# Row sums of a 16384 x 1024 array: the last two rows in shared column pieces, one row for each engine, and ScalarE as the engine that stores

## Chip, core and metric

One core of one Trainium2 chip. The metric is device time in microseconds (us), best read as the median of several executions. "Faster" or "slower" would need 2%, that is 3.3 us. In the tables, times inside one execution count from the start of its span, at the first load's issue. The batches of runs were on different chips, by the record, so a time is compared within its batch; the traces are one execution of each kernel.

## The reference

```python
x = np.random.randn(32, 512, 1024).astype(np.float32)
def reference(x):
    return np.sum(x, axis=-1).astype(np.float32)
```

67.1 MB are read, 64 KB are written, and there is one addition for each number read.

## The kernel before

Each of the 128 partitions owns 128 rows, in 8 groups of 16. Groups 0 to 6 are one load each (16 rows of 4 KB, 64 KB for each partition). VectorE (DVE) sums them with one reduce; in group 6 ScalarE (ACT) takes half, with a Copy activation for each row whose accumulator output is the sum and whose elementwise output nobody reads. Group 7 is the tail. It comes in loads of 8, 4, 2, 1 rows and a last row in three column pieces, so that little is left to do when the last byte has landed.

```python
    nbig = J // BIG - 1                       # 7; BIG = 16
    tail = [(8, 4), (4, 2), (2, 1)]           # (rows, rows for ScalarE)
    ...
        def act(dst, src, n):
            nc.scalar.activation(out=scratch[:, :n], in_=src, func=Copy, accum_out=dst)
    ...
        for i in range(nbig):
            t = inpool.tile([P, BIG * dim + 2], fp32)
            rows_of(t, 0, BIG, i * BIG, BIG // 2 if i == nbig - 1 else 0)
            if i % 3 == 2:
                store(nc.gpsimd, i - 2, i + 1)
        store(nc.gpsimd, nbig - 1, nbig)
        ...                                   # loads and sums of 8, 4, 2 rows
        rows_of(t, a, 1, nbig * BIG + a, 1)   # row 14: ScalarE alone
        a += 1
        j = nbig * BIG + a                    # row 15: DVE alone, three pieces
        last = t[:, a * dim :]
        cuts = [0, 384, 768, dim]
        for c0, c1 in zip(cuts, cuts[1:]):
            nc.sync.dma_start(out=last[:, c0:c1], in_=rows_from(j, 1)[:, 0, c0:c1])
        for i, (c0, c1) in enumerate(zip(cuts, cuts[1:])):
            if c1 < dim:                      # partial sum goes right behind the row
                vec(last[:, dim + i : dim + i + 1], last[:, c0:c1])
            else:                             # last piece and both partial sums at once
                vec(sums[:, j : j + 1], last[:, c0 : dim + i])
        store(nc.sync, nbig, nbig + 1)
```

`scratch` is a single tile in SBUF (SBUF and PSUM are two memories on the chip, from which the tile pools take their buffers). The stores of groups 0 to 6 are issued by GpSimd (POOL), the last one by the sync engine (SP).

Of the kernel before, what the change touches and what calls it, by code (L numbers as in the profile page):

```python
# [1 line left out]

# [4 lines left out]


def issue_first_load_at_entry(nc):

    main, *rest = nc.main_func.blocks
    SP = mybir.EngineType.SP
    for block in rest:
        insts = list(block.instructions)
        at = next(
            (k for k, i in enumerate(insts) if isinstance(i, mybir.InstDMACopy) and i.engine == SP),
            None,
        )
        if at is None:
            continue  # L20
        load = insts.pop(at)
        assert not load.sync_info.on_wait
        block.instructions = insts
        entry = list(main.instructions)
        k = next(k for k, i in enumerate(entry) if isinstance(i, mybir.InstDrain) and i.engine == SP)
        main.instructions = entry[:k] + [load] + entry[k:]
        return


@with_exitstack  # L30
def kernel(
    ctx: ExitStack,
    tc: tile.TileContext,
    x: bass.AP,
    out: bass.AP,
):
    nc = tc.nc
    nc.at_finalize(issue_first_load_at_entry)
    fp32 = mybir.dt.float32
    P = 128  # L40
    batch, seq, dim = x.shape
    rows = batch * seq
    J = rows // P
    BIG = 16


    x_g = x.flatten_outer_dims().rearrange("(g p j) d -> g p j d", p=P, j=BIG)
    out_v = out.rearrange("b s -> (b s)").rearrange("(g p j) -> p g j", p=P, j=BIG)

    def rows_from(j, n):  # L50
        return x_g[j // BIG, :, j % BIG : j % BIG + n, :]


    nbig = J // BIG - 1
    tail = [(8, 4), (4, 2), (2, 1)]

    with (
        tc.tile_pool(name="in", bufs=3) as inpool,
        tc.tile_pool(name="scratch", bufs=1) as spool,
        tc.tile_pool(name="stage", bufs=1) as stpool,  # L60
    ):
        sums = stpool.tile([P, J], fp32)
        scratch = spool.tile([P, dim], fp32)

        def vec(dst, src):
            nc.vector.tensor_reduce(  # L66
                out=dst, in_=src, axis=mybir.AxisListType.X, op=mybir.AluOpType.add
            )

        def act(dst, src, n):  # L70
            nc.scalar.activation(  # L71
                out=scratch[:, :n],
                in_=src,
                func=mybir.ActivationFunctionType.Copy,
                accum_out=dst,
            )

        def rows_of(t, a, n, j, n_act):
            nv = n - n_act
            block = t[:, a * dim : (a + n) * dim].rearrange("p (n d) -> p n d", d=dim)  # L80
            nc.sync.dma_start(out=block, in_=rows_from(j, n))  # L81
            if nv:
                vec(sums[:, j : j + nv], block[:, :nv, :])
            for q in range(nv, n):
                act(sums[:, j + q : j + q + 1], block[:, q, :], dim)

        def store(eng, g0, g1):
            eng.dma_start(  # L88
                out=out_v[:, g0:g1],
                in_=sums[:, g0 * BIG : g1 * BIG].rearrange("p (g j) -> p g j", j=BIG),  # L90
            )

        for i in range(nbig):
            t = inpool.tile([P, BIG * dim + 2], fp32)
            rows_of(t, 0, BIG, i * BIG, BIG // 2 if i == nbig - 1 else 0)

            if i % 3 == 2:
                store(nc.gpsimd, i - 2, i + 1)
        store(nc.gpsimd, nbig - 1, nbig)

        t = inpool.tile([P, BIG * dim + 2], fp32)
        a = 0
        for n, n_act in tail:
            rows_of(t, a, n, nbig * BIG + a, n_act)
            a += n


        rows_of(t, a, 1, nbig * BIG + a, 1)
        a += 1
        j = nbig * BIG + a  # L110
        last = t[:, a * dim :]
        cuts = [0, 384, 768, dim]
        for c0, c1 in zip(cuts, cuts[1:]):
            nc.sync.dma_start(out=last[:, c0:c1], in_=rows_from(j, 1)[:, 0, c0:c1])
        for i, (c0, c1) in enumerate(zip(cuts, cuts[1:])):
            if c1 < dim:
                vec(last[:, dim + i : dim + i + 1], last[:, c0:c1])
            else:
                vec(sums[:, j : j + 1], last[:, c0 : dim + i])
        store(nc.sync, nbig, nbig + 1)  # L120


# [1 line left out]
_INS = ['x']  # L124
_OUTS = [((32, 512), 'float32')]


# [23 lines left out]
```

## Time and profile before

Median 162.79 us of 3 runs at first. The profiled execution has a span of 161.5 us.

First the page of the profile: the slice rows (busy share in tenths, 40 equal slices of the span) and the DMA queues (packets, MB, share of 16 engines' span).

```profile
DVE  0000049998699968999499994999949997697883
DMA  8997998997997997996996996996997996999990
q1 hardware_dynamic: 2160, 67.12, 97.1%
q0 software_dynamic: 96, 0.06, 0.1%
```

The load queue (q1) is busy for 97.1% of the span on all sixteen engines. The packet records say the same: the median load packet of 65,536 B takes 2.418 us, which is about 434 GB/s for sixteen engines; the first 16 packets take longer, 3.57 us in the mean. DVE is idle for the first five slices, until the first 16 rows have landed, and waits for loads again later.

Next, the end of the timeline (start us, duration us, engine, line, operation, output<-input, count, and in brackets the idle time before it and what ended it).

```profile
157.09 1.06 ACT L71 ACTIVATE scratch<-t 128x1024 f32<-128x1024 f32 x1
157.64 1.01 DVE L66 TENSOR_REDUCE t<-t 128x1 f32<-128x384 f32 x2 [0.68 <-DMA t<-in_x_dram]
158.06 0.19 ACT L71 ACTIVATION_READ_ACCUMULATOR scratch<-t 128x1 f32 x1
158.68 0.42 DVE L66 TENSOR_REDUCE sums<-t 128x1 f32<-128x258 f32 x1
159.17 0.35 SPq L88 DMA_DIRECT2D out_dram<-sums  x1
```

The second line is two merged reduces, one for each of the first two pieces. Beside it stand the landings by the semaphore records of the same trace (a semaphore is a counter that a transfer or an instruction raises when it is done, and that others wait for): the pieces landed at 157.54, 158.05 and 158.37 us. So the final reduce began 0.31 us after the last landing: DVE was still at the second piece. The final store was issued at 159.17 and landed at 160.59; 0.95 us later the span ends.

The last pieces of the chain of waits (start us, duration us, what) tell the same story from the back: one DMA stretch of 38.6 us, then two partial reduces, then the final one.

```profile
118.95 38.59 DMA t<-in_x_dram
...
157.64 1.02 DVE t L66 x2
158.66 0.02 issue
158.68 0.42 DVE sums L66
```

### The profile page before, as it was taken

How to read it: one execution, taken by the hardware profiler on the slowest of the kernel's cores; microseconds unless marked ns; L12 is line 12 of the kernel's file. 1: busy time of each engine (PE TensorE's matmuls, PEld its weight loads, DVE VectorE, ACT ScalarE, POOL GpSimd, SP SyncE). 2: the span in 40 equal slices, each digit the busy share in tenths (PEclk: the TensorE clock that was granted, in tenths of full speed). 3: DMA queues.
4: the chain of work that ended last, by engine and by line, in shares of the span. 5: the costliest groups of instructions: out<-in, count | busy, mean ns of one | idle time of the engine just before them, and what ended most of it. 6: DMA issues, size and time to landing. Idle time of an engine off the chain costs nothing.

```text
span 161.5 us, 124 instructions
## 1 busy us (share of the span) xinstructions
DVE 121.4 (75%) x13; ACT 19.7 (12%) x33; POOL 2.4 (1%) x7
## 2 busy tenths in 40 slices
DVE  0000049998699968999499994999949997697883
ACT  3000000000000000000000000000000000698891
POOL 0000000000000000000200000000000001001000
DMA  8997998997997997996996996996997996999990
GB/s 260 519 438 341 519 406 373 519 438 341 519 454 325 519 471 308 519 487 292 519 493 293 519 487 292 519 487 292 519 454 325 519 487 292 391 491 389 410 392 14
DMA packets 2256, 67.18 MB, mean 416 GB/s; under 512 B 416, under 2 KB 848, under 8 KB 976
## 3 DMA queue, kind: packets, MB, share of 16 engines
q1 hardware_dynamic: 2160, 67.12, 97.1%
q0 software_dynamic: 96, 0.06, 0.1%
HBM read 67.11 MB, written 0.07 MB: 416 GB/s over the span
## 4 chain that ended last, share of the span: by engine, by line
DMA 74%; DVE 22%; SPq 1%; issue 0%; DVEq 0%
DMA t<-in_x_dram 74%; DVE sums L66 22%; SPq L81 1%; DVE t L66 1%; DVEq L66 0%
## 5 line engine op out<-in xcount | busy, mean ns | idle before, releaser
L66 DVE TENSOR_REDUCE sums<-t 128x16 f32<-128x16384 f32 (+5 forms) x11 | 120.4, 10941 | 37.1 <-DMA t<-in_x_dram 37.0
L71 ACT ACTIVATE scratch<-t 128x1024 f32<-128x1024 f32 x16 | 16.9, 1057 | 137.8 <-DMA t<-in_x_dram 137.3
L88 POOL DMA_DIRECT2D out_dram<-sums x3 | 2.2, 732 | 146.2 <-DVE sums L66 135.4
L71 ACT ACTIVATION_READ_ACCUMULATOR scratch<-t 128x1 f32 x16 | 3.0, 186 | 0.0
L66 DVE TENSOR_REDUCE t<-t 128x1 f32<-128x384 f32 x2 | 1.0, 549 | 0.7 <-DMA t<-in_x_dram 0.7
L71 ACT ACT_TABLE_LOAD x1 | 1.3, 1283 | 0.8 <-PEq L135 0.8
L135 POOL MEMSET const-float32-0.0<- 128x1 f32 x1 | 0.1, 98 | 0.2 <-issue 0.2
L135 POOL MEMSET const-bfloat16-1.0<- 128x1 bf16 x1 | 0.1, 101 | 0.0
L135 POOL MEMSET const-uint8-127<- 128x1 uint8 x1 | 0.1, 99 | 0.0
L135 POOL MEMSET const-float32-1.0<- 128x1 f32 x1 | 0.1, 98 | 0.0
## 6 DMA issues: line engine op xcount, KB each, us to landing
t<-in_x_dram SPq DMA_DIRECT2D x1, 4096.0 KB, 31.2
t<-in_x_dram SPq DMA_DIRECT2D x1, 2048.0 KB, 35.9
t<-in_x_dram SPq DMA_DIRECT2D x1, 1024.0 KB, 37.8
t<-in_x_dram SPq DMA_DIRECT2D x1, 512.0 KB, 38.6
t<-in_x_dram SPq DMA_DIRECT2D x2, 192.0 KB, 38.6
t<-in_x_dram SPq DMA_DIRECT2D x1, 128.0 KB, 38.4
t<-in_x_dram SPq DMA_DIRECT2D x7, 40.8
out_dram<-sums POOLq DMA_DIRECT2D x2, 24.0 KB, 7.9
```

Source lines behind the costliest of these rows:

```text
L66: nc.vector.tensor_reduce(out=dst, in_=src, axis=mybir.AxisListType.X, op=mybir.AluOpType.add)
L71: nc.scalar.activation(out=scratch[:, :n], in_=src, func=mybir.ActivationFunctionType.Copy, accum_out=dst,)
L81: nc.sync.dma_start(out=block, in_=rows_from(j, n))
L88: eng.dma_start(out=out_v[:, g0:g1], in_=sums[:, g0 * BIG : g1 * BIG].rearrange("p (g j) -> p g j", j=BIG),)
L135: nc = _bacc.Bacc("TRN2", target_bir_lowering=False, num_devices=1)
```

## The change

The intent: share the last two rows between the engines, so that both work on the end of the stream at once; take POOL out of the kernel; put the store of groups 1 to 6 where it hides under the end of the tail; and issue a first, early store from ScalarE. The diff, cut to its core:

```diff
-    tail = [(8, 4), (4, 2), (2, 1)]
+    pieces = (640, 256, 128)
-        tc.tile_pool(name="scratch", bufs=1) as spool,
+        tc.tile_pool(name="unread", bufs=4, space=bass.MemoryType.PSUM) as upool,
+        tc.manual_schedule(),
         def act(dst, src, n):
+            unread = upool.tile([P, dim], fp32)
             nc.scalar.activation(
-                out=scratch[:, :n],
+                out=unread[:, :n],
@@ groups 0 to 6
-            if i % 3 == 2:
-                store(nc.gpsimd, i - 2, i + 1)
-        store(nc.gpsimd, nbig - 1, nbig)
+            if g == 1:
+                store(nc.scalar, 0, 1)       # ScalarE's first instruction
@@ tail: 8, 4, 2 rows as before; then, in place of row 14 and row 15
+        for width in pieces:                 # each piece: both rows
+            if len(parts) == k:              # k = 2; room before the last piece
+                at += k
+            part = t[:, at : at + 2 * width].rearrange("p (n d) -> p n d", n=2)
+            nc.sync.dma_start(out=part, in_=rows_from(j, 2)[:, :, c : c + width])
+            ...
+        w = t[:, at - 2 * width - k : at + k]
+        for i, part in enumerate(parts[:k]): # row 14: DVE, row 15: ScalarE
+            vec(w[:, i : i + 1], part[:, 0, :])
+            act(w[:, k + 2 * width + i : k + 2 * width + i + 1], part[:, 1, :], pieces[i])
+        store(nc.scalar, 1, last)
+        vec(sums[:, j : j + 2], w.rearrange("p (n d) -> p n d", n=2))
         store(nc.sync, last, last + 1)
```

In the buffer, DVE's partial sums stand before the last piece of row 14 and ScalarE's behind the last piece of row 15. One reduce of 2 x 130 columns therefore finishes both rows; it has to wait for ScalarE. The change also brings `tc.manual_schedule()`, program order.

More of the change, by code (lines that the diff above doesn't have):

```diff
@@ L51, in rows_from @@
         return x_g[j // BIG, :, j % BIG : j % BIG + n, :]
-    nbig = J // BIG - 1
-    tail = [(8, 4), (4, 2), (2, 1)]
+    last = J // BIG - 1
+    pieces = (640, 256, 128)
     with (
         tc.tile_pool(name="in", bufs=3) as inpool,
-        tc.tile_pool(name="scratch", bufs=1) as spool,
+        tc.tile_pool(name="unread", bufs=4, space=bass.MemoryType.PSUM) as upool,
         tc.tile_pool(name="stage", bufs=1) as stpool,
+        tc.manual_schedule(),
     ):
         sums = stpool.tile([P, J], fp32)
-        scratch = spool.tile([P, dim], fp32)
         def vec(dst, src):
@@ L76, in act, with rows @@
             )
-        def rows_of(t, a, n, j, n_act):
+        def rows(t, a, n, j, n_act):
             nv = n - n_act
@@ L81, in rows_of @@
             nc.sync.dma_start(out=block, in_=rows_from(j, n))
-            if nv:
-                vec(sums[:, j : j + nv], block[:, :nv, :])
+            vec(sums[:, j : j + nv], block[:, :nv, :])
             for q in range(nv, n):
@@ L91, in store @@
             )
-        for i in range(nbig):
-            t = inpool.tile([P, BIG * dim + 2], fp32)
-            rows_of(t, 0, BIG, i * BIG, BIG // 2 if i == nbig - 1 else 0)
-            if i % 3 == 2:
-                store(nc.gpsimd, i - 2, i + 1)
-        store(nc.gpsimd, nbig - 1, nbig)
-        t = inpool.tile([P, BIG * dim + 2], fp32)
+        for g in range(last):
+            t = inpool.tile([P, BIG * dim + 4], fp32)
+            rows(t, 0, BIG, g * BIG, BIG // 2 if g == last - 1 else 0)
+            if g == 1:
+                store(nc.scalar, 0, 1)
+        t = inpool.tile([P, BIG * dim + 4], fp32)
         a = 0
-        for n, n_act in tail:
-            rows_of(t, a, n, nbig * BIG + a, n_act)
+        j = last * BIG
+        for n in (8, 4, 2):
+            rows(t, a, n, j + a, n // 2)
             a += n
-        rows_of(t, a, 1, nbig * BIG + a, 1)
-        a += 1
-        j = nbig * BIG + a
-        last = t[:, a * dim :]
-        cuts = [0, 384, 768, dim]
-        for c0, c1 in zip(cuts, cuts[1:]):
-            nc.sync.dma_start(out=last[:, c0:c1], in_=rows_from(j, 1)[:, 0, c0:c1])
-        for i, (c0, c1) in enumerate(zip(cuts, cuts[1:])):
-            if c1 < dim:
-                vec(last[:, dim + i : dim + i + 1], last[:, c0:c1])
-            else:
-                vec(sums[:, j : j + 1], last[:, c0 : dim + i])
-        store(nc.sync, nbig, nbig + 1)
+        j += a
+        at = a * dim
+        k = len(pieces) - 1
+        parts = []
+        c = 0
+        for width in pieces:
[3 more added lines that the diff above has]
+            nc.sync.dma_start(out=part, in_=rows_from(j, 2)[:, :, c : c + width])
+            parts.append(part)
+            at += 2 * width
+            c += width
+        w = t[:, at - 2 * width - k : at + k]
[4 more added lines that the diff above has]
+        vec(sums[:, j : j + 2], w.rearrange("p (n d) -> p n d", n=2))
+        store(nc.sync, last, last + 1)
 _INS = ['x']
```

## The prediction

> **What bounds it.** The load stream. The slice table has DMA at 9 or near it in every slice, the queue table gives the load queue 97.1% of sixteen engines' span, and single packet records show no gaps: a 65,536 B packet takes 2.418 us on each of 16 engines, 433 GB/s together. The Trainium skill ("DMA: Bandwidth & Descriptors", Specifications) names a fabric ceiling of 435 GB/s; this trace agrees. So the stream's end (last byte landed 158.37 us into the span of 161.5) is fixed by bytes plus packet overhead, and only the 3.2 us behind it can move. DVE (75% busy) and ACT (12%) wait for loads nearly everywhere (waits view).
>
> **The tail before.** Semaphore records, us into the span: row 14 lands at 157.01, the pieces of row 15 (384, 384, 256 columns) at 157.54, 158.05, 158.37. The timeline and chain of waits have DVE reducing piece 1 at 157.64, piece 2 at 158.11, and the final 258 columns at 158.68 (0.42 us). So DVE starts the final reduce 0.31 us after the last landing; at most that is there to be won. Store issued 159.17, landed about 160.6, then about 0.9 us of closing barrier.
>
> **What the change does to it.**
> - Stream. From packet records (4096 B 159 ns, 1536 B 65, 1024 B 46, 512 B 27; so 2560 B about 103, an estimate): per engine, rows 14 and 15 cost 8x159+16x66+8x47 = 2.70 us before, 16x103+16x46+16x27 = 2.82 after: +0.1. The POOL stores leave the stream (184 ns per engine, measured); the early ScalarE store adds about 0.1. Net within 0.1 us of zero.
> - Landings after (estimate): 640 columns at about 157.3, 256 at 158.05, 128 at 158.45.
> - DVE: 640 takes 0.15+1.04x640 ns = 0.82 (line through 0.42 at 258 and 1.22 at 1024): 157.4 to 158.2; 256 to 158.65.
> - ACT: one activation of N columns with its accumulator read is 1.18 us from start to start at 1024. The Trainium skill ("ScalarE: Activation LUTs", What ACT_TABLE_LOAD costs) gives 0.833 ns per element plus a fixed part; 1057 ns at 1024 here fits. So 640: 157.37 to 158.2; 256: to 158.73. Writing to PSUM may save some tens of ns.
> - The final reduce (2x130 = 260 columns) thus starts at 158.7 to 158.8 instead of 158.68: the tail is as limited by the middle pieces' compute as before. Gain about 0; my centre is +0.1.
> - The late ScalarE store of groups 1 to 6 (768 rows of 64 B, about 0.5 us of packets per engine at 11 ns) is issued about 158.3, some 1 us before the final store, and should land just before it (160.3 against 160.7). If issuing 768 descriptors is slow, or the final store queues behind it, up to about 1 us is lost: the main risk.
> - Moving the table load (1.28 us, at 0.78) behind the early store changes nothing: ACT first works at 138.5. A small chance: all 16 first packets take about 3.6 us instead of 2.4 while the table loads; were that the cause, 1 us would be won. I take it for start-up latency.
>
> **Predicted:** 162.9 us (before 162.79), range 162.4 to 163.6. Within 2%: 0.98; faster or slower by over 2%: 0.01 each.
>
> **What would show it.** Right: last load landing within 0.15 us of before; final reduce starting 0.25 to 0.4 us after it, released by ACT; final store issue to landing 1.4 us; first packets still near 3.6 us. Wrong: ScalarE's store landing after the final store, or the final store taking over 1.6 us (slower); ACT done before DVE's 256 piece with the last landing earlier (faster); first packets of 2.4 us (faster).

## The result

The changed kernel took 162.86 us (median of 4, 162.76 to 163.08), against 162.82 us before (median of 4). The ratio is 1.0001 with a 95% interval of 0.9984 to 1.0018. Here and below a ratio is the mean time of one kernel's runs over that of the other's in the same batch, so not quite the ratio of the medians. Run again beside other kernels, it was 162.92 against 162.95 us, ratio 0.9997 (0.9984 to 1.0010).

The page of the changed kernel, the lines that answer to those of before:

```profile
DVE  0000059997799959999499994999949998697883
DMA  8996996996996996997998998998998998998992
q1 hardware_dynamic: 2400, 67.12, 97.3%
q10 hardware_dynamic: 928, 0.06, 0.4%
```

The load queue is as full as before. The POOL queue q0 is gone; q10 is ScalarE's, with ten times the packets for about the same bytes: there are now 896 packets of 64 B where POOL's stores had 48 of 512 or 1,536 B.

The end of its timeline:

```profile
157.28 1.15 DVE L67 TENSOR_REDUCE t<-t 128x1 f32<-128x640 f32 x2 [0.50 <-DMA t<-in_x_dram]
157.34 0.71 ACT L73 ACTIVATE unread<-t 128x640 f32<-128x640 f32 x1 [0.57 <-DMA t<-in_x_dram]
157.99 0.19 ACT L73 ACTIVATION_READ_ACCUMULATOR unread<-t 128x1 f32 x1
158.08 0.37 ACT L73 ACTIVATE unread<-t 128x256 f32<-128x256 f32 x1
158.17 0.39 ACTq L89 DMA_DIRECT2D out_dram<-sums  x1
158.39 0.19 ACT L73 ACTIVATION_READ_ACCUMULATOR unread<-t 128x1 f32 x1
158.60 0.42 DVE L67 TENSOR_REDUCE sums<-t 128x2 f32<-128x260 f32 x1 [0.17 <-ACT unread L73]
159.06 0.36 SPq L89 DMA_DIRECT2D out_dram<-sums  x1
```

The pieces landed at 157.19, 157.98 and 158.34 us. Both engines start on the first piece at 157.3. DVE is through with its partial sums at 158.43, ScalarE at 158.57, and the bracket of the final reduce says that ScalarE released it. It starts 0.27 us after the last landing, 0.04 us sooner than before. The late store (ACTq) is issued before all that is over and landed at 160.15, ahead of the final store at 160.48. The DMA view gives issue to landing:

```profile
out_dram<-sums ACTq DMA_DIRECT2D x1, 48.0 KB, 2.0
out_dram<-sums ACTq DMA_DIRECT2D x1, 8.0 KB, 23.9
out_dram<-sums SPq DMA_DIRECT2D x1, 8.0 KB, 1.4
```

To add up what changed, I cut the end of each execution at events that all kernels have, by the semaphore and instruction records. "Row 13" is the landing of the two-row load, "last" that of the last piece.

| us | before | changed | difference |
|---|---|---|---|
| row 13 to last landing (rows 14 and 15 on the stream) | 2.657 | 2.796 | +0.139 |
| last landing to start of final reduce | 0.312 | 0.268 | -0.044 |
| final reduce | 0.421 | 0.423 | +0.002 |
| its end to landing of final store | 1.487 | 1.449 | -0.038 |
| that landing to end of span | 0.945 | 0.813 | -0.132 |
| sum | 5.822 | 5.749 | -0.073 |

So the tail's loads got longer by about as much as the closing part got shorter, and the final reduce hardly moved. What remains is less than the spread of one kernel's runs: the kernel before ran from 162.71 to 163.65 us within 11 runs. Most effects below are of this size, so they are shown by the traces and not by the times.

### The profile page after: what moved, and what is told of

It reads as the page before. It is cut to its first block, busy times and chain, and to the rows that moved or that the text cites. A ratio compares the mean times of both kernels' runs of the same rounds, so it can differ in the third digit from the quotient of the medians.

```text
span 161.3 us, 124 instructions
## 1 busy us (share of the span) xinstructions
DVE 121.5 (75%) x13; ACT 18.5 (11%) x35; POOL 0.2 (0%) x4
## 4 chain that ended last, share of the span: by engine, by line
DMA 75%; DVE 22%; SPq 1%; issue 0%; ACTq 0%; ACT 0%; DVEq 0%
DMA t<-in_x_dram 75%; DVE sums L67 22%; SPq L83 1%; DVE t L67 1%; ACTq L89 0%; ACT unread L73 0%; DVEq L67 0%
## 5 line engine op out<-in xcount | busy, mean ns | idle before, releaser
L73 ACT ACTIVATE unread<-t 128x1024 f32<-128x1024 f32 (+2 forms) x17 | 16.2, 955 | 100.3 <-DMA t<-in_x_dram 100.3
L73 ACT ACTIVATION_READ_ACCUMULATOR unread<-t 128x1 f32 x17 | 3.2, 186 | 0.0
L67 DVE TENSOR_REDUCE t<-t 128x1 f32<-128x640 f32 (+1 forms) x2 | 1.1, 615 | 0.5 <-DMA t<-in_x_dram 0.5
```

The source lines that it names most:

```text
L67: nc.vector.tensor_reduce(out=dst, in_=src, axis=mybir.AxisListType.X, op=mybir.AluOpType.add)
L73: nc.scalar.activation(out=unread[:, :n], in_=src, func=mybir.ActivationFunctionType.Copy, accum_out=dst,)
```

## The experiments

My theory was that nothing large hides here. The stream's end is fixed; the start of the final reduce is set by the compute of the middle pieces, so sharing them wins almost nothing; and the stores are off the critical path. The rivals: two large effects cancel (the tail wins, the stores lose or the other way round); or the early store or the moved table load matter by themselves. Two more questions came up on the way: what a store of many 64 B packets costs beside the load stream, and what made ScalarE faster.

This table has the parts named above for every run (us, one profiled execution each), then the median time and the ratio to the kernel before with its interval.

| run | row 13 to last | last to final | end of reduce to landing | landing to end | sum | median, ratio |
|---|---|---|---|---|---|---|
| before | 2.66 | 0.31 | 1.49 | 0.95 | 5.82 | |
| changed, first | 2.80 | 0.27 | 1.45 | 0.81 | 5.75 | 162.86, 1.0001 |
| a_tail_only | 2.81 | 0.46 | 1.47 | 1.00 | 6.16 | 163.45, 1.0019 (0.9998-1.0039) |
| b_stores_only | 2.68 | 0.31 | 1.48 | 0.85 | 5.74 | 162.80, 0.9981 (0.9959-1.0004) |
| c_no_early | 2.81 | 0.29 | 1.46 | 0.88 | 5.86 | 162.82, 0.9981 (0.9961-1.0000) |
| d_mid_store | 2.77 | 0.28 | 1.46 | 0.81 | 5.76 | 162.90, 0.9986 (0.9966-1.0007) |
| e_after_again | 2.81 | 0.29 | 1.46 | 0.82 | 5.80 | 162.92, 0.9997 (0.9984-1.0010) |
| f_sbuf_scratch | 2.80 | 0.43 | 1.45 | 0.82 | 5.92 | 162.92, 1.0004 (0.9989-1.0020) |
| g_four_pieces | 2.92 | 0.19 | 1.46 | 0.79 | 5.79 | 162.94, 1.0002 (0.9986-1.0019) |
| h_one_store | 2.78 | 0.33 | 2.20 | 0.94 | 6.66 | 163.56, 1.0042 (1.0028-1.0056) |
| i_mix | 2.77 | 0.22 | 1.49 | 0.81 | 5.72 | 162.77, 0.9988 (0.9976-1.0000) |
| j_first_split | 2.82 | 0.29 | 1.46 | 0.79 | 5.78 | 163.08, 0.9997 (0.9982-1.0011) |
| k_psum_one | 2.79 | 0.44 | 1.46 | 0.81 | 5.93 | one look |
| m_sbuf_three | 2.79 | 0.30 | 1.46 | 0.81 | 5.79 | one look |

The sum includes the final reduce, 0.42 us in all of them. All results were correct. Kernels a to d shared one set of runs of the kernel before (median 163.14 us), e to h one (162.95), i and j one (162.97).

### a_tail_only: the new tail, the old stores and scratch

```diff
 kernel before:
-        rows_of(t, a, 1, nbig * BIG + a, 1)  # ... and row 15 in three pieces
+        # the two-row pieces of the change, word for word
```

> The two-row tail alone; stores stay on POOL, ScalarE keeps writing one SBUF scratch. My theory (the change nets zero because the stream's end is fixed and the middle pieces' compute decides when the final reduce starts): final reduce starts 0.35 to 0.45 us after the last landing, released by ScalarE (0.31 in the kernel before, 0.27 in the changed one), span ends 3.15 to 3.35 us after the last landing, time within 0.3 us of the kernel before. Rival (two large effects cancel: the tail wins, the stores lose): 0.4 us or more faster than before, span ending under 2.9 us after the last landing.

The tail alone did not win: the sum is 0.34 us longer than before and the median 0.3 us higher, though the interval still touches 1. The final reduce starts 0.46 us after the last landing; I had expected 0.35 to 0.45, and the span ends 3.35 us after the last landing, at the edge of the expected 3.15 to 3.35. The timeline, without the accumulator reads:

```profile
157.67 1.15 DVE L67 TENSOR_REDUCE t<-t 128x1 f32<-128x640 f32 x2 [0.56 <-DMA t<-in_x_dram]
157.73 0.74 ACT L72 ACTIVATE scratch<-t 128x640 f32<-128x640 f32 x1 [0.58 <-DMA t<-in_x_dram]
158.59 0.42 ACT L72 ACTIVATE scratch<-t 128x256 f32<-128x256 f32 x1
159.13 0.42 DVE L67 TENSOR_REDUCE sums<-t 128x2 f32<-128x260 f32 x1 [0.32 <-ACT scratch L72]
```

ScalarE's second activation starts 0.86 us after its first here, 0.74 us after it in the changed kernel (157.34 to 158.08), and DVE sits idle 0.32 us for it. So the new tail needs the faster ScalarE to break even. What makes it faster is settled below.

### b_stores_only: ScalarE's stores and PSUM, the old tail

```diff
 kernel before:
-                store(nc.gpsimd, i - 2, i + 1)   # and the one of group 6
+                store(nc.scalar, 0, 1)           # if i == 1
@@ before the final store
+        store(nc.scalar, 1, nbig)
```

> ScalarE's two stores, PSUM target and program order alone; the tail of the kernel before. My theory: final reduce starts 0.31 us after the last landing as before, the span ends 3.0 to 3.1 us after it (the closing part about 0.13 us shorter, as in the changed kernel), time within 0.3 us of before. Rival (stores lose what the tail wins): 0.4 us or more slower, with the final store over 1.6 us from issue to landing.

As my theory had it: the final reduce at 0.31 us, the closing part 0.09 us shorter than before, the final store 1.42 us from issue to landing. The signs of a and b are opposite, so there is some cancelling, but in the traces of effects of 0.1 to 0.3 us. The times are less sharp: b's median is 0.34 us below that of the kernel before, slightly more than the 0.3 that I had allowed, with 1 inside its interval. Kernels c and d of the same batch are 0.2 to 0.3 us below it too, so much of that may be a high median of the kernel before in this batch. The tail does not win 0.4 us, and the stores do not lose it; some cancelling of a few tenths the other way round is not excluded by the times.

### c_no_early: without the early store

```diff
 changed kernel:
-            if g == 1:
-                store(nc.scalar, 0, 1)
-        store(nc.scalar, 1, last)
+        store(nc.scalar, 0, last)
```

> The changed kernel without the early store: one late ScalarE store of seven groups, the first transfer of its queue, and the table load back at the start. If the early store warms the queue up: the late store takes well over 2.0 us from issue to landing (3 us or more), lands after the final store, and the time grows by 0.5 us or more. My theory (no warm-up needed): issue to landing 2.0 to 2.2 us, the final store still ends last, time within 0.2 us of the changed kernel. Table-load theory: if the early table load slows the first 16 packets, they take about 3.6 us again against 3.2 in the changed kernel; otherwise they lie anywhere between.

```profile
out_dram<-sums ACTq DMA_DIRECT2D x1, 56.0 KB, 2.1
out_dram<-sums SPq DMA_DIRECT2D x1, 8.0 KB, 1.4
```

The late store, now the first transfer of its queue, took 2.1 us instead of 2.0 with seven groups instead of six. No warm-up shows. Where the table load stands makes no difference to the first 16 packets either: their mean is 2.96, 2.99, 3.13 and 3.11 us in runs a, c, h and i, where it runs at the start, and 2.98, 3.21, 3.13, 3.00 and 3.14 us in runs b, d, e, f and g, where it runs near 39.6 us. So the 3.57 us in the profile of the kernel before is not explained by where the table load stands; the other traces with this load have 2.96 to 3.21 us.

### d_mid_store: the late store inside the load stream

```diff
 changed kernel:
+        store(nc.scalar, 1, last)      # here: right after group 6
         t = inpool.tile([P, BIG * dim + 4], fp32)
         a = 0
 ...
-        store(nc.scalar, 1, last)
```

> The changed kernel with the store of groups 1 to 6 issued as soon as their sums exist (at about 147 us), inside the load stream. My theory (a store of 64 B packets costs the stream its packets' own time, 48 per engine at about 11 ns): last landing about 0.5 us later counted from the landing of the last 16-row load, time 0.3 to 0.6 us longer; final store 1.4 us from issue to landing, as in the changed kernel, which shows that the late store does not hold it up. Rival (bytes count, not packets): 48 KB at the stream's rate is 0.1 us, no measurable change.

```profile
out_dram<-sums ACTq DMA_DIRECT2D x1, 48.0 KB, 11.0
out_dram<-sums ACTq DMA_DIRECT2D x1, 8.0 KB, 23.7
out_dram<-sums SPq DMA_DIRECT2D x1, 8.0 KB, 1.4
```

Here my own expectation failed. From the landing of the last 16-row load to the last landing it is 19.94 us; the runs with the same tail and no store there have 19.89 to 20.06 (the changed kernel, c, e, f, h). The store's packet records in the load stream add up to 0.54 us for each engine, and none of it is to be seen in the stream's length. The same holds in run i below, with 0.62 us of records: 19.90 us, against 19.87 in run b with the same tail and no store there. Adding up packet records of two queues as if they stood in one line, as I did here and in the prediction, does not give the time here. What absorbs the small packets is left open. That bytes alone count agrees with the result, but 48 KB would be only 0.1 us, which this run cannot resolve.

The 11.0 us and the 23.7 us have a visible reason. The early store has 128 packets of 64 B, 8 for each of 16 engines. Their records come in rounds of 16, most of them about 2.4 us apart, the time of one load packet of 64 KB (which engine carried a packet is not in the trace). The Trainium skill ("DMA: Bandwidth & Descriptors", Queues, rings and completion order) says that an engine goes round its queues and switches only at packet boundaries; the trace agrees.

### e_after_again, f_sbuf_scratch, k_psum_one, l_sbuf_four, m_sbuf_three: what made ScalarE faster

```diff
 e: the changed kernel, as it is
 f:  -name="unread", bufs=4, space=PSUM     +name="scratch", bufs=1 (SBUF), one tile for all
 k:  -name="unread", bufs=4, space=PSUM     +name="unread", bufs=1, space=PSUM
 l:  -name="unread", bufs=4, space=PSUM     +name="unread", bufs=4 (SBUF)
 m:  -name="unread", bufs=4, space=PSUM     +name="unread", bufs=3 (SBUF)
```

> The changed kernel once more, as a control beside the next three. Final reduce 0.25 to 0.30 us after the last landing, span ending 2.9 to 3.05 us after it, time within 0.3 us of the kernel before.

> The changed kernel with ScalarE writing one SBUF scratch again, as the kernel before does. My theory (with one scratch each activation waits for the one before it, and that decides when the final reduce starts): start to start of 1024-column activations 1.18 us again instead of 1.04; final reduce 0.40 to 0.47 us after the last landing, as in the tail-only run (0.46), so 0.15 to 0.2 us later than the control; span ending 3.1 to 3.2 us after the last landing. Rival (the stores, not the activations, made the tail-only run's end late): final reduce about 0.27 us after the last landing, as in the control.

> The changed kernel with one PSUM buffer instead of four. If the four buffers give ScalarE its speed (an activation need not wait for the one before): start to start of 1024-column activations is about 1.15 to 1.18 us again, and the final reduce starts 0.40 to 0.45 us after the last landing. If PSUM itself gives it: 1.04 us and 0.27 to 0.29 us.

> The changed kernel with four buffers in SBUF instead of PSUM. If the four buffers give ScalarE its speed: start to start about 1.04 to 1.07 us and the final reduce 0.27 to 0.33 us after the last landing. If PSUM itself gives it: 1.18 us and 0.43 us.

> The changed kernel with three buffers in SBUF instead of four in PSUM (four do not fit). If several buffers give ScalarE its speed: start to start of 1024-column activations about 1.04 to 1.07 us, and the final reduce 0.27 to 0.33 us after the last landing. If it takes PSUM as well: start to start nearer 1.18 us and 0.40 us or more.

Kernel l did not build: beside three input tiles, four buffers of 4 KB do not fit into a partition of SBUF (16 KB wanted, 15.75 KB left). Kernel m took its place.

ScalarE's lines of the timelines at the start of group 6, first k (one PSUM buffer), then m (three SBUF buffers):

```profile
137.95 1.03 ACT L73 ACTIVATE unread<-t 128x1024 f32<-128x1024 f32 x1 [97.16 <-DMA t<-in_x_dram]
138.91 0.19 ACT L73 ACTIVATION_READ_ACCUMULATOR unread<-t 128x1 f32 x1
139.13 1.03 ACT L73 ACTIVATE unread<-t 128x1024 f32<-128x1024 f32 x1
```

```profile
138.26 1.06 ACT L73 ACTIVATE unread<-t 128x1024 f32<-128x1024 f32 x1 [97.13 <-DMA t<-in_x_dram]
139.22 0.19 ACT L73 ACTIVATION_READ_ACCUMULATOR unread<-t 128x1 f32 x1
139.32 1.04 ACT L73 ACTIVATE unread<-t 128x1024 f32<-128x1024 f32 x1
```

With one buffer the next activation starts when the accumulator read is over, 1.18 us after the one before it, in PSUM (k) as in SBUF (f). With several buffers it starts while that read still runs, after 1.06 us for the first two and 1.04 us later on, in SBUF (m) as in PSUM (the changed kernel). PSUM itself shortens only the activation's record, 1.03 instead of 1.06 us; the accumulator read begins 0.96 us after the start in either case. The instruction records show what it waits for. With one buffer every activation after the first carries a wait for the semaphore that ScalarE's own accumulator reads raise. With several, the activations behind the first carry none until the buffers have all been used once (from the fifth on with four, from the fourth on with three). So the wait comes with the reuse of a buffer.

The final reduce follows: 0.43 and 0.44 us after the last landing with one buffer (f, k), 0.27 to 0.30 with several (the changed kernel, e, m). The lines of the final reduce, first f, then its control e:

```profile
158.28 0.42 DVE L68 TENSOR_REDUCE sums<-t 128x2 f32<-128x260 f32 x1 [0.32 <-ACT scratch L73]
```

```profile
158.35 0.43 DVE L67 TENSOR_REDUCE sums<-t 128x2 f32<-128x260 f32 x1 [0.17 <-ACT unread L73]
```

So the number of buffers is the cause, and PSUM is where four of them had room. The gain is seen in the traces alone: the medians of f and e are both 162.92 us. In f the stores are those of the changed kernel, so the rival that blamed the stores for run a falls.

### g_four_pieces: another cut of the last two rows

```diff
 changed kernel:
-    pieces = (640, 256, 128)
+    pieces = (512, 256, 128, 128)
```

> The changed kernel with the last two rows in four pieces of 512, 256, 128 and 128 columns. My theory (the middle piece's compute decides when the final reduce starts, and each piece costs the stream 16 packets' fixed part per engine): final reduce 0.10 to 0.17 us after the last landing instead of 0.27, and the time from the landing of row 13 to the last landing 2.94 us instead of 2.80 (16 packets each of 84, 46, 27 and 27 ns, an estimate from the line through the packet times), so no net gain. Rival (a wait of fixed length after the last landing): final reduce again 0.27 us after it, and the time 0.14 us longer.

```profile
157.85 0.28 ACT L73 ACTIVATE unread<-t 128x128 f32<-128x128 f32 x1
157.90 0.39 ACTq L89 DMA_DIRECT2D out_dram<-sums  x1
158.06 0.19 ACT L73 ACTIVATION_READ_ACCUMULATOR unread<-t 128x1 f32 x1
158.28 0.43 DVE L67 TENSOR_REDUCE sums<-t 128x2 f32<-128x262 f32 x1 [0.21 <-ACT unread L73]
```

The last landing was at 158.09 us. The final reduce starts 0.19 us after it, 0.10 us sooner than in the control e, and not because of a fixed wait: with less middle work it moved, still released by ScalarE. It missed my 0.10 to 0.17 a little. The stream pays for the extra piece: row 13 to last landing is 2.92 us, against 2.81 in the control and 2.94 expected. The sums are 5.79 and 5.80 us: nothing gained. This is one exchange of stream time for waiting time, measured with one extra piece.

### h_one_store: all sums in the final store

```diff
 changed kernel:
-            if g == 1:
-                store(nc.scalar, 0, 1)
-        store(nc.scalar, 1, last)
-        store(nc.sync, last, last + 1)
+        store(nc.sync, 0, last + 1)
```

> The changed kernel with no ScalarE store at all: the final store writes all eight groups. My theory (the late ScalarE store is hidden under the last reduces and the final store): the final store now has 64 packets of about 10 ns per engine instead of 8, so 1.9 to 2.2 us from issue to landing instead of 1.4, and the span ends 3.4 to 3.7 us after the last landing; time about 0.5 us longer than the control. Rival (a store's latency is fixed): 1.4 us and no longer than the control.

```profile
out_dram<-sums SPq DMA_DIRECT2D x1, 64.0 KB, 2.2
```

It is the one kernel whose interval lies wholly on the slow side of 1: 0.64 us over the control by the medians. The store takes 2.2 us instead of 1.4. The span ends 3.89 us after the last landing, more than the 3.4 to 3.7 that I expected, since the closing part was longer as well. In the other kernels the late store is therefore hidden work, not free work.

### i_mix: an attempt to beat both

```diff
 b_stores_only:
-                store(nc.scalar, 0, 1)
-        store(nc.scalar, 1, nbig)      # before the final store
+        store(nc.scalar, 0, nbig)      # right after group 6
```

> An attempt to beat both: the tail of the kernel before (shorter stream: 2.66 to 2.68 us from the landing of row 13 to the last landing, against 2.80), ScalarE writing PSUM, and one ScalarE store of seven groups inside the stream at about 147 us, since the run with that store there lost nothing. If the terms add as measured: final reduce 0.30 us after the last landing, span ending 2.95 to 3.05 us after it, about 0.1 us less than the changed kernel from the landing of row 13 to the end, and a time that cannot be told from it (within 0.15 us). Rival (bigger effects are still hidden): 0.4 us or more away from the changed kernel either way.

162.77 against 162.97 us, ratio 0.9988 with an interval that ends at 1.0000. It has the shortest sum of all, 5.72 us, as expected about 0.1 less than the changed kernel's second run. But it is not shown to be faster, and at 0.1% it would hardly matter. One thing was not as expected: its store of seven groups was still in progress in the tail (it landed at 158.07, after the last load at 157.90), and there row 13 to last landing was 2.77 us instead of the 2.68 of run b. The final reduce followed the last landing 0.08 us sooner for it.

### j_first_split: the first load in two

```diff
 changed kernel, group 0:
-            nc.sync.dma_start(out=block, in_=rows_from(j, n))
+            # rows 0-1, then rows 2-15
```

> The changed kernel with its first load cut into 2 rows (8 KB packets) and 14 rows. In all runs so far the first 16 packets of 64 KB take 2.9 to 3.6 us instead of 2.42, wherever the table load stands. If that is a start-up delay of each engine: the first 8 KB packets take about 0.31 us plus 0.5 to 0.8 us each, and the first 16 rows land no earlier than in the control (21.8 to 22.0 us), time unchanged within 0.2 us. If large first packets are themselves slow: the first 16 rows land 0.5 us or more earlier, and the time falls by as much.

Inconclusive. The first 16 packets, now 8 KB, took 0.36 to 1.10 us instead of 0.31, so most of the excess stands with small packets as well, as a start-up delay would have it. The first 16 rows landed at 21.66 us, against 21.80 to 22.00 in the other timed runs of the changed kernel and its variants: a gain of 0.1 to 0.3 us that the time (ratio 0.9997) does not show. This execution lost 0.8 us in the middle of the stream: from the landing of group 0 to that of group 6 it took 116.9 us, against 116.1 to 116.2 in nine of the other eleven traces of timed kernels (the two others: the changed kernel's first with 116.4, a with 116.8). There, load packets take up to 2.7 us instead of 2.42 for some microseconds. This happens with and without stores nearby; its cause is open. In the profiled executions it goes with longer times: 163.22 us in j, 163.81 in a and 163.08 in the changed kernel's first, against 162.63 to 162.84 in b to g and i.

## Why the prediction was right

The time was predicted as 162.9 us in a range of 162.4 to 163.6; it measured 162.86. Point by point:

- **The stream bounds it, and its end hardly moves.** Right. The last landing was at 158.34 against 158.37 us. That these two are so close is partly luck: the changed execution started 0.4 us faster and lost 0.3 us in the middle. The safe reading is row 13 to the last landing, +0.14 us for a predicted +0.12. The line through the packet durations (about 8 ns for each packet plus 0.037 ns for each byte) was good enough for that; 2,560 B took 102 ns for an estimated 103.
- **The other stream terms.** The prediction charged the stream 0.18 us for POOL's stores and 0.1 us for the early one. These nearly cancelled, so it did no harm, but in runs d and i such records, added to the stream of loads, gave a delay that did not come.
- **The final reduce waits for ScalarE, 0.25 to 0.4 us after the last landing.** Right: 0.27 and 0.29 us in two runs, released by ScalarE. Run g moves it by changing the middle pieces, f and k by slowing ScalarE.
- **ScalarE's speed.** The reason given was wrong: "Writing to PSUM may save some tens of ns." PSUM saved nothing that counts; four buffers instead of one saved 0.14 us from start to start at 1024 columns. Without that the final reduce would have come at 0.43 us (f), outside the predicted range. The range was hit partly by luck. The prediction had ScalarE take 1.36 us from its start on the first piece to its end, which is right for one buffer (1.37 in f) but not for four (1.23). It also let ScalarE start 0.07 us after the first landing where the traces have 0.16. The two errors nearly cancelled.
- **The late store is hidden; the main risk did not come true.** Right: it landed at 160.15 (predicted 160.3), the final store at 160.48 (160.7). Issuing 768 rows of 64 B took ScalarE's queue 0.39 us, hardly more than the 0.36 us of SP's 128.
- **The table load.** Right to take it for no cause of slow first packets: runs a, c, h, i against b, d to g. But the sign named for it, "first packets still near 3.6 us", did not come: the changed kernel's have a mean of 3.12 us, and the runs with the table load at the start 2.96 to 3.13.
- **The closing part, "about 0.9 us", was missed as a term.** It fell from 0.95 to 0.81 us. Two things are visible in the records. SP makes one wait fewer after the final landing (one wait is about 0.06 us; the runs have 0 to 3 of them, by where the final store's semaphore happens to stand in SP's list). And POOL's closing drain and semaphore clear take 70 + 93 ns instead of 101 + 136 ns; the clear is 136 ns in the two kernels in which POOL issues stores (before, a) and 93 ns in all others. Why is not shown.

## What to carry to other kernels

In this kernel, where the load stream fills the DMA engines, a finer tail only traded one term for another: in run g one more piece made the stream 0.11 us longer and the wait behind the last landing 0.10 us shorter. Look at what releases the last instruction: here it was ScalarE, and a rotating output buffer that nobody reads was worth more to it than the split itself (0.14 us, in the traces alone). And try small stores where something else is running: here they showed no cost in the stream or under the last reduces, and alone at the end they cost 0.6 us (run h).

## What the Trainium skill lacked or had wrong

- "ScalarE: Activation LUTs" (Step-by-step: what each stage is for; the tip that ScalarE to PSUM is faster than to SBUF): true of the activation's record here, 1.03 against 1.06 us at 1024 columns, but with an accumulator output it gained nothing from start to start (1.18 us in both with one buffer, 1.04 in both with several).
- The same page (What ACT_TABLE_LOAD costs) says that back-to-back activations overlap by about 93 ns. With an accumulator output the changed kernel has the same 93 ns as the time by which an activation starts before the accumulator read of the one before ends. The page lacks that such an activation brings a read of 186 ns behind it, and that the overlap is lost when each activation writes the buffer of the one before: with the wait, 0.14 us more from start to start.
- "DMA: Bandwidth & Descriptors" (Specifications): its fabric ceiling of 435 GB/s agrees with about 434 GB/s here. It lacks what small stores cost beside a full stream of loads: 48 packets of 64 B for each engine, 0.54 us of packet records, lengthened the stream by nothing visible (run d).
- The same page (Queues, rings and completion order) has the switching at packet boundaries, but not how long a turn can be: a load packet of 64 KB takes 2.42 us here, and an 8 KB store with 8 packets for each engine beside such loads took 23.9 us to land.
- "Runtime: NRT & Kernel Launch" deals with what the runtime puts around a kernel. It lacks, as do the pages drawn on above, the close that the program itself brings: 0.79 to 1.00 us from the final store's landing to the end of the span, of which about 0.06 us is for each semaphore wait of SP still to come.
